# A decoder layer between its first layer norm and its feed-forward: where the sums of the Strassen operands run, how many pairs begin ahead, when the first weights are split, and how many buffers the norm's output has

## The chip, the cores and the metric

The kernel runs on one core of one Trainium2 chip. The metric is device time in microseconds (us) of one execution, the median of three runs. TensorE (PE) does the matrix products, VectorE (DVE) and ScalarE (ACT) the elementwise work, GpSimd (POOL) a little of it, and SyncE (SP) issues nearly all transfers.

## The reference

One layer of a hybrid decoder on 1056 tokens (1024 of a prompt and 32 of samples), 1024 wide, in float32. Attention and an mLSTM head group come first; the change lies behind them:

```python
mixed = jnp.concatenate([h_ml, o_nsa], axis=-1) @ w_out
x = layer_norm(ALPHA * x + g1 * mixed, ln_g[0], ln_b[0])
u2 = x * (1 + sc2) + sh2
ff = jnp.square(jax.nn.relu(u2 @ w_up)) @ w_down
x = layer_norm(ALPHA * x + g2 * ff, ln_g[1], ln_b[1])
```

`w_up` is 1024 x 4096 and `w_down` 4096 x 1024.

## The kernel before, in words

**Precision.** TensorE multiplies in a reduced float32. Each operand is therefore split into a high and a low part (`split`, L50 and L51: ScalarE rounds the high part, VectorE subtracts it from the source), and each product is three products: high by high, high by low, low by high.

**Norm.** Tokens are worked in three chunks `c` of 384, 384 and 288. `wout_steps(c)` multiplies the mixed heads by `w_out`; `ln1(c)` turns the result by TensorE transposes (`pn`), normalises it by rows (`xn`), turns it back (`pb`), scales it on ScalarE into a tile `x1` of two rotating buffers (L1303), stores that (`d_x1`, L1304) for the second residual, and makes `u2` from it in `uraw` (L1307 to L1310). Then it splits the quarters of `uraw` that are operands as they stand.

**Feed-forward up.** `u2 @ w_up` is done by a Strassen-Winograd scheme: two halves of the features by two halves of the tokens give the blocks B11, B21 and B22 and the sums T1 to T4, and seven products make a pair `p` of weight tiles (16 pairs; one weight tile is 512 KB). Two of the seven take B11 and B21 alone, and need no sum:

```python
def first_products(p, ra, v1):
    for x, of in multiply(p, 1, w_of(p, "11", ra[:, 0:4]), "B11"):
        ACT.copy(of(v1), x)
    combine(p, v1, multiply(p, 2, w_of(p, "12", ra[:, 4:8]), "B21"), 0, 0)
```

The other five, in `up_pair`, take T2, T1, T3, B22 and T4 in that order. The sums are T3 = B22 - T3's own quarter, T2 = T3 + its quarter, T4 = its quarter - T2, T1 = B22 - T2, each in place in `uraw`. Before, T3 and T2 are made inside `ln1` for chunks 1 (on GpSimd, 240 columns) and 2 (on VectorE, 288 columns); T4 and T1 later, whole (528 columns, four instructions each), on GpSimd (`TENG`, L1364 records all of them). `t_step` makes and splits one of the four operands.

**Pairs begun ahead.** Of the first `NF` = 4 pairs the two products without a sum are done ahead: those of pairs 0 and 1 inside the norm (`up_early`, with weights split there), those of pairs 2 and 3 after it (`up_start`, tile names `wpre` and `aws`), each followed by a `t_step`. Their result `V1` goes to memory (`d_v1`) and is read again when the pair's other five products run; their weight tile is read again too. `wpre`, the weights of pair 2, is loaded early, but split after the norm into tiles (`a`, four buffers each of high and low) of a pool that opens when the norm's pools close. Other weight tiles share three buffers (`aw`).

**Order.** Instructions are emitted in the order of the program; at build a planner with a simulated time line may start a later one earlier on an engine that would stand idle, and so fixes one order for each engine's queue and for SP's transfers. That is why rows of one line are interleaved with rows of others below.

Of the kernel before, what the change touches and what calls it, by code (L numbers as in the profile page):

```python
# [22 lines left out]
F32 = mybir.dt.float32  # L23
F32R = mybir.dt.float32r
# [12 lines left out]
EPS = 1e-5  # L37
GC = math.sqrt(2.0 / math.pi)
TH, HH = T // 2, T // 4
NF = 4  # L40
KT, B22L = 0, True
NE = 2


# [3 lines left out]
def split(nc, hi, lo, src):  # L48

    nc.scalar.copy(hi, src)  # L50
    nc.vector.tensor_tensor(out=lo, in0=src, in1=hi.bitcast(F32), op=ALU.subtract)  # L51


def body(tc, io, dbg=None):
    with ExitStack() as top:
        _body(tc, tc.nc, top, io, dbg or {})


def _body(tc, nc, top, io, dbg):
    PE, ACT, DVE, POOL, SP = nc.tensor, nc.scalar, nc.vector, nc.gpsimd, nc.sync  # L60

    def pool(name, stack, bufs=1, space=None, side=None):
        kw = {}
        if space is not None:
            kw["space"] = space
        if side is not None:
            kw["side"] = side
        if space is not DRAM:
            kw["reuse_waits"] = "tile"
        return stack.enter_context(tc.tile_pool(name=name, bufs=bufs, **kw))  # L70

    def mk(p, shape, dt, tag, bufs=None, name=None):
        kw = {} if bufs is None else {"bufs": bufs}
        return p.tile(list(shape), dt, tag=tag, name=name or tag, **kw)
# [16 lines left out]
    def v4(x, t=4):  # L91
        return x.rearrange("p (b t) -> p b t", t=t)

    def bc(x, n):

        return x.unsqueeze(2).broadcast_to([x.shape[0], x.shape[1], n])
# [729 lines left out]
    for h in range(2):  # L826
# [23 lines left out]
        for j in range(2):  # L850
            o, p = 512 * j, 288 * j
# [321 lines left out]
    while not (qs.end and qp.end and dn_end):  # L1173
# [4 lines left out]
        if best <= t and (behind or dn_at > t):  # L1178
            if rp <= t:
                qp.need = None  # L1180
                c = qp.pull()
            else:
                qs.need = None
                c = qs.pull()
# [4 lines left out]
        elif dn_at <= t:  # L1189
            x = next(dense, None)  # L1190
# [6 lines left out]
        else:  # L1197
            if fill is None and heads_done[0] and filled < 2 and blocks_done[0] >= 11 + 3 * filled:
                fill = wout_steps(filled)
            if fill is not None:  # L1200
                x = next(fill, None)
# [25 lines left out]
    ops = {}  # L1227

    def operand(pp, name):
        ops[name] = tuple(mk(pp, [128, 4, TH], F32R, name + x) for x in "hl")  # L1230
# [8 lines left out]
    p4 = pool("p4", s4_, side="right")  # L1239
# [20 lines left out]
    def norm_rows(pp, pts, name, cols, rows):  # L1260

        xn, st = norm_tiles(pp, name)
        for hf in range(2):
            norm_half(pts, st, cols, hf, rows)
        _, r, nmr = norm_stats(st, rows)
        for hf in range(2):
            ACT.activation(xn[0:rows, 512 * hf:512 * hf + 512], pts[hf][0:rows], AF.Identity, scale=r, bias=nmr)
        return xn
# [22 lines left out]
    def ln1(c):  # L1291
        t0, n = CH[c]
        tts = [(o, min(128, n - o)) for o in range(0, n, 128)]
        xns = []
        for o, rows in tts:
            pts = [mk(ps4, [128, 512], F32, "t", bufs=4, name=f"pn{c}{o}{hf}") for hf in range(2)]
            xns.append(norm_rows(p4, pts, f"a{c}{o}", [ys[c, m][:, o:o + rows] for m in range(8)], rows))
        for f in range(8):
            pt = mk(ps4, [128, 512], F32, "t2", bufs=2, name=f"pb{c}{f}")
            for (o, rows), xn in zip(tts, xns):  # L1300
                PE.transpose(pt[:, o:o + rows], xn[0:rows, 128 * f:128 * f + 128], ident[0:rows, 0:rows])
            x1 = mk(p4, [128, 384], F32, "x1", bufs=2, name=f"x1{c}{f}")
            ACT.activation(x1[:, 0:n], pt[:, 0:n], AF.Identity, scale=lnT[:, 0, f:f + 1], bias=lnT[:, 1, f:f + 1])  # L1303
            SP.dma_start(d_x1[:, f, t0:t0 + n], x1[:, 0:n])  # L1304
            u = uraw[:, f, t0:t0 + n]
            np_ = min(n, 1024 - t0)
            DVE.tensor_scalar(u[:, 0:np_], x1[:, 0:np_], sc2p[:, f, 0:1], ada[:, 3, f, 0:1], op0=ALU.mult, op1=ALU.add)  # L1307
            if np_ < n:
                DVE.tensor_tensor(out=v4(u[:, np_:n]), in0=v4(x1[:, np_:n]), in1=bc(sc2p[:, f, 1:9], 4), op=ALU.mult)
                DVE.tensor_tensor(out=v4(u[:, np_:n]), in0=v4(u[:, np_:n]), in1=bc(ada[:, 3, f, 1:9], 4), op=ALU.add)  # L1310
            for a, b, name in ((t0, min(t0 + n, TH), "B21" if f >= 4 else "B11"), (max(t0, TH), t0 + n, "B22")):
                if a < b and (a < TH or f >= 4 and c < 2):
                    hi, lo = (x[:, f % 4, a % TH:a % TH + b - a] for x in ops[name])
                    split(nc, hi, lo, uraw[:, f, a:b])
            if f >= 4 and c:
                a, b = ((0, 240), (240, TH))[c - 1]
                t_sum("T3", f - 4, a, b, POOL if c == 1 else DVE)
                t_sum("T2", f - 4, a, b, POOL if c == 1 else DVE)
                if c == 2 and f < 4 + KT:
                    split(nc, ops["T2"][0][:, f - 4], ops["T2"][1][:, f - 4], ublock("T2", f - 4, 0, TH))  # L1320

    d_r = [mk(dr, [128, 2, T], F32, f"d_r{p}") for p in range(16)]
    d_v1 = [mk(dr, [128, TH], F32, f"d_v1{p}") for p in range(NF)]

    def product(ps, w, name, h):

        for i, (a, b) in enumerate(((0, 0), (0, 1), (1, 0))):
            for k in range(4):
                PE.matmul(ps[:, 0:HH], lhsT=w[a][:, k], rhs=ops[name][b][:, k, HH * h:HH * h + HH],  # L1329
                          start=(i == 0 and k == 0), stop=(i == 2 and k == 3))  # L1330
# [19 lines left out]
    def relu2(x):  # L1350
        DVE.scalar_tensor_tensor(out=x, in0=x, scalar=0.0, in1=x, op0=ALU.max, op1=ALU.mult)
# [6 lines left out]
    def ublock(name, k, a, b):  # L1358
        f, t = blk[name]
        return uraw[:, f + k, t + a:t + b]  # L1360

    def t_sum(name, k, a, b, eng):
        x, y, op = sum_of[name]
        eng.tensor_tensor(out=ublock(name, k, a, b), in0=ublock(x, k, a, b), in1=ublock(y, k, a, b), op=op)  # L1364

    TENG = POOL
    ln1(0)
    for _ in fill or wout_steps(1):
        pass
    ln1(1)  # L1370
    for _ in wout_steps(2, pq):
        pass
    operand(pq, "T2")
    ln1(2)
    spre = ExitStack()
    ppre = pool("pre", spre)
    wpre = mk(ppre, [128, 8, 128], F32, "wpre")
    if NF > NE:
        SP.dma_start(wpre, io["w_up"][2 * NE].rearrange("p (k c) -> p k c", k=8))
    for p in range(NE):  # L1380
        up_early(p)
    s4_.close()
# [13 lines left out]
        operand(pT, name)  # L1396

    def t_split(name, a=0):
        for k in range(KT if name == "T2" else 0, 4):
            split(nc, ops[name][0][:, k, a:], ops[name][1][:, k, a:], ublock(name, k, a, TH))  # L1400

    ns = [0]
# [1 line left out]
    def slot(name):  # L1404

        ns[0] += 1
        if ns[0] % 2:
            t = mk(psd, [128, 2, 512], F32, "d", bufs=2, name=name)
            return [t[:, h] for h in range(2)], [(t[:, :, 0:HH], lambda x: x.rearrange("p (h c) -> p h c", h=2))]
        ts = [wtile(f"{name}{h}") if ns[0] % 4 else mk(psd, [128, 512], F32, "t", bufs=2, name=f"{name}{h}") for h in range(2)]  # L1410
        return ts, [(t[:, 0:HH], lambda x, h=h: x[:, HH * h:HH * h + HH]) for h, t in enumerate(ts)]

    def w_of(p, name, src):
        hl = [mk(pU, [128, 4, 128], F32R, "a" + x, bufs=4, name=f"a{x}{p}{name}") for x in "hl"]
        split(nc, *hl, src)
        return hl

    def multiply(p, name, w, op):
        ps, pieces = slot(f"p{name}{p}")
        for h in range(2):  # L1420
            product(ps[h], w, op, h)
        return pieces

    def add(out, v, ps):
        for x, of in ps:
            DVE.tensor_tensor(out=of(out), in0=of(v), in1=x, op=ALU.add)

    def combine(p, v, ps, f, half):

        c = mk(pU, [128, TH], F32, "C", bufs=2, name=f"C{p}{f}{half}")  # L1430
        add(c, v, ps)
        relu2(c)
        SP.dma_start(d_r[p][:, f, TH * half:TH * half + TH], c)

    def first_products(p, ra, v1):
        for x, of in multiply(p, 1, w_of(p, "11", ra[:, 0:4]), "B11"):
            ACT.copy(of(v1), x)
        combine(p, v1, multiply(p, 2, w_of(p, "12", ra[:, 4:8]), "B21"), 0, 0)

    def up_start(p):  # L1440
        ra = wpre
# [7 lines left out]
    def up_pair(p):  # L1449
# [5 lines left out]
        def tile_(tag, bufs=1):  # L1455
            return mk(pU, [128, TH], F32, tag, bufs=bufs, name=f"{tag}{p}")

        v1 = tile_("V1", 2)
        if p < NF:
            SP.dma_start(v1, d_v1[p])  # L1460
# [15 lines left out]
    def t_step(op):  # L1476
        if op == "T1" and B22L:
            t_split("B22", 240)
        if op not in ("T2", "T3"):
            for k in range(4):  # L1480
                t_sum(op, k, 0, TH, TENG)
        t_split(op)

    steps = ["T2", "T3", "T4", "T1"]
    for p in range(NE, NF):
        up_start(p)
        if steps:
# [380 lines left out]
```

## Time and profile before

| | |
|---|---|
| median of three runs | 1561.07 us (1560.75 to 1563.67) |
| profiled execution, its own time | 1566.92 us |
| its span | 1565.1 us |
| mean granted TensorE clock | 0.981 of full speed |
| TensorE busy | 95% of the span |

The profiled execution is 5.85 us longer than the median of the runs, and 1.8 us of its time lie outside the span. A busy TensorE row is modelled time: two rows overlap at their ends, and at a low granted clock the same matmul is longer.

### The profile page before, as it was taken

The page shows a single profiled execution, that of the slowest core. Times are in us where ns is not written, and L with a number is a line of the kernel's source. Part 1 is how long each engine was busy: PE and PEld are TensorE (multiplying, and loading weights), DVE is VectorE, ACT ScalarE, POOL GpSimd, SP SyncE. Part 2 cuts the span into 40 slices and gives each one's busy share as a digit, 9 for nine tenths or more (in the row PEclk, how much of TensorE's full clock was granted, in tenths as well). Part 3 has the DMA queues.
Part 4 walks back from the last instruction along what each step waited for, and adds up shares of the span by engine and source line. Part 5 has one row for each costly group of instructions (what it writes and reads, how often), then busy time and mean ns, then how long its engine had stood idle before and what let it go on. Part 6 is the DMA issues. An engine that isn't in the chain of part 4 may idle for free.

```text
span 1565.1 us, 30108 instructions
## 1 busy us (share of the span) xinstructions
PE 1491.6 (95%) x11647; PEld 1434.5 (92%) x11647; DVE 1029.1 (66%) x2347; ACT 657.3 (42%) x1332; POOL 254.3 (16%) x386
## 2 busy tenths in 40 slices
PE   6899999999999999999998799999999999999985
PEld 5789988899999998798897799999999999999984
DVE  2521131386676777977688887667668687879856
ACT  2422132375565666745366422222225533334443
POOL 0000000143223233443102400000000000002132
PEclk9999999999999999999999799999999999999998
DMA  8766576421020323233464476333324452526473
GB/s 301 272 212 243 134 195 224 146 67 59 26 78 18 82 82 121 80 66 107 155 214 143 164 233 207 125 110 109 105 82 142 141 166 71 150 97 138 111 133 112
DMA packets 115722, 212.04 MB, mean 135 GB/s; under 512 B 18834, under 2 KB 63803, under 8 KB 114651
## 3 DMA queue, kind: packets, MB, share of 16 engines
q1 hardware_dynamic: 109242, 196.67, 39.0%
q0 software_dynamic: 5040, 12.13, 4.7%
q8 instruction: 92, 1.51, 0.4%
q10 hardware_dynamic: 1296, 1.31, 0.2%
q14 instruction: 52, 0.42, 0.1%
HBM read 162.95 MB, written 46.07 MB: 134 GB/s over the span
## 4 chain that ended last, share of the span: by engine, by line
PE 80%; DMA 8%; DVE 6%; issue 2%; ACT 2%; SPq 1%; POOL 0%; ACTq 0%; DVEq 0%; POOLq 0%
PE p L1329 20%; PE pd L1564 18%; PE pj L354 16%; PE po L354 6%; PE o L1060 4%; PE pt L1019 4%; PE S L979 4%; DMA wada<-in_w_ada 3%; DMA xk<-in_xT 1%; PE pA L298 1%; PE ada L149 1%; PE pd L1664 1%; DMA xnf<-ln 1%; PE hidS L277 1%; PE S L983 1%
## 5 line engine op out<-in xcount | busy, mean ns | idle before, releaser
L1564 PE MATMUL pd<-oplT,ophT 128*128 128x264 f32 x2352 | 288.3, 285 | 0.0
L1564 PEld LDWEIGHTS pd<-oplT,ophT 128*128 128x128 f32 x2352 | 288.0, 188 | 0.1
L1002 POOL TENSOR_SCALAR P<-P,l,sg 128x64 f32<-128x64 f32 (+8 forms) x192 | 128.2, 681 | 178.2 <-DVE l L999 159.4
L996 ACT ACTIVATE P<-P,mn 128x640 f32<-128x640 f32 (+7 forms) x128 | 94.3, 737 | 69.8 <-DVE mn L823 66.3
L51 DVE TENSOR_TENSOR PTl<-pt,PTh 128x512 fp32r<-128x512 f32 (+1 forms) x160 | 101.7, 642 | 28.7 <-ACT PTh L50 28.4
L354 PE MATMUL pj<-uh,wt_l 128*128 128x384 f32 (+1 forms) x576 | 120.2, 333 | 0.0
L50 ACT CAST PTh<-pt 128x512 fp32r<-128x512 f32 (+1 forms) x160 | 86.5, 549 | 78.6 <-PE pt L1019 77.9
L354 PE MATMUL pj<-uh,wt_h 128*128 128x384 f32 (+1 forms) x576 | 115.8, 331 | 1.7 <-ACT rw L468 1.7
L354 PE MATMUL pj<-ul,wt_h 128*128 128x384 f32 (+1 forms) x576 | 116.3, 329 | 0.0
L50 ACT CAST ophT<-A 128x1024 fp32r<-128x1024 f32 x49 | 51.2, 1049 | 117.5 <-PE pd L1564 107.4
L354 PEld LDWEIGHTS pj<-uh,wt_l 128*128 128x128 f32 x576 | 95.6, 190 | 2.9 <-issue 2.4
L354 PEld LDWEIGHTS pj<-uh,wt_h 128*128 128x128 f32 x576 | 93.5, 188 | 4.2 <-ACT rw L468 2.0
L1019 PE MATMUL pt<-ident,P 128*128 128x128 f32 x592 | 95.9, 276 | 1.1 <-POOL P L1002 1.0
L354 PEld LDWEIGHTS pj<-ul,wt_h 128*128 128x128 f32 x576 | 94.4, 188 | 1.9 <-issue 1.4
L1615 POOL DMA_DIRECT2D A<-A x7 | 6.3, 895 | 525.4 <-DVE ophT L51 525.4
L1569 DVE TENSOR_TENSOR acc<-acc,pd 128x264 f32<-128x264 f32 (+1 forms) x126 | 62.0, 514 | 28.5 <-PE pd L1564 28.3
L1060 PE MATMUL o<-PTh,V 128*128 128x256 f32 x264 | 79.2, 307 | 0.4 <-DVE ob L1079 0.4
L1060 PE MATMUL o<-PTl,V 128*128 128x256 f32 x264 | 72.7, 296 | 3.1 <-DVE PTl L51 2.7
L1019 PEld LDWEIGHTS pt<-ident,P 128*128 128x128 f32 x592 | 70.4, 141 | 4.3 <-POOL P L1002 1.8
L979 PE MATMUL S<-K,QH 128*128 128x512 f32 (+3 forms) x200 | 71.9, 363 | 0.9 <-DVE mn L823 0.7
L51 DVE TENSOR_TENSOR ophT<-A,ophT 128x1024 fp32r<-128x1024 f32 x49 | 59.6, 1219 | 11.5 <-ACT ophT L50 11.5
L50 ACT CAST ah<-aw 128x512 fp32r<-128x512 f32 x40 | 24.8, 621 | 94.4 <-PE p L1329 94.4
(1104 smaller groups left out, 3473.2 us busy)
## 6 DMA issues: line engine op xcount, KB each, us to landing
wada<-in_w_ada SPq DMA_DIRECT2D x48, 512.0 KB
aw<-in_w_up SPq DMA_DIRECT2D x32, 512.0 KB
d_r<-C SPq DMA_DIRECT2D x62, 264.0 KB
B<-d_r SPq DMA_DIRECT2D x28, 528.0 KB
A<-in_w_down SPq DMA_DIRECT2D x28, 512.0 KB
wst<-in_w_t SPq DMA_DIRECT2D x24, 512.0 KB
wst<-in_w_out SPq DMA_DIRECT2D x24, 512.0 KB
w<-in_cmp_w SPq DMA_DIRECT2D x4, 1024.0 KB
```

The source lines that it names most:

```text
L50: nc.scalar.copy(hi, src)
L51: nc.vector.tensor_tensor(out=lo, in0=src, in1=hi.bitcast(F32), op=ALU.subtract)
L149: PE.matmul(ps[32 * j:32 * j + 32, 0:128], lhsT=sil[:, k, :], rhs=w[:, k % 2, j], start=(k == 0), stop=(k == 7), tile_position=(0, 32 * j))
L354: PE.matmul(ps[:, 0:n], lhsT=a[:, k, :], rhs=b[:, k, t0:t0 + n], start=(i == 0 and k == 0), stop=(i == 2 and k == 7))
L979: PE.matmul(S[:, 0:w], lhsT=Q[:, r], rhs=K[j][:, k0 + c0:k0 + c0 + w], start=(i == 0), stop=(i == 1))
L996: ACT.activation(P[:, o:o + n], P[:, o:o + n], AF.Exp, bias=mn[:, br:br + 1], scale=-1.0, accum_out=l[:, br:br + 1])
L1002: POOL.tensor_scalar(P[:, a:b], P[:, a:b], l[:, x:x + 1], sg[:, qb, y:y + 1], op0=ALU.mult, op1=ALU.mult)
L1019: PE.transpose(pt[:, 256 * x + 128 * e:256 * x + 128 * e + 128], P[:, o:o + 128], ident)
L1060: PE.matmul(op, lhsT=vv, rhs=ps[e][:, 256 * x:256 * x + 256], start=(x0 + x == 0 and e == 0), stop=(x0 + x == len(bl) - 1 and e == 1))
L1329: PE.matmul(ps[:, 0:HH], lhsT=w[a][:, k], rhs=ops[name][b][:, k, HH * h:HH * h + HH], start=(i == 0 and k == 0), stop=(i == 2 and k == 3))
L1564: PE.matmul(ps[h][:, 0:HH], lhsT=x[:, 128 * m:128 * m + 128], rhs=y[:, HH * h:HH * h + HH], start=(i == 0), stop=(i == len(mms) - 1))
L1569: DVE.tensor_tensor(out=out, in0=out, in1=x, op=ALU.add)
```

## The change

Operand sums leave GpSimd: T3 and T2 are no longer made inside `ln1` but after it, in two pieces each on VectorE, and T4 and T1 are made on VectorE. `NF` becomes 6, so that the first two products of pairs 2 to 5 are done ahead of pair 0's other five. `wpre` is emitted before the norm, and its split, as one instruction on ScalarE and one on VectorE into tiles of its own, before the norm's last chunk. `x1` has six buffers in place of two. The order of the operands becomes T2, T1, T3, T4, the order in which the pair uses them. (`KT` was 0, so its lines did nothing.)

```diff
-NF = 4
-KT, B22L = 0, True
+NF = 6
+B22L = True
...
-            x1 = mk(p4, [128, 384], F32, "x1", bufs=2, name=f"x1{c}{f}")
+            x1 = mk(p4, [128, 384], F32, "x1", bufs=6, name=f"x1{c}{f}")
...
-            if f >= 4 and c:
-                a, b = ((0, 240), (240, TH))[c - 1]
-                t_sum("T3", f - 4, a, b, POOL if c == 1 else DVE)
-                t_sum("T2", f - 4, a, b, POOL if c == 1 else DVE)
-                if c == 2 and f < 4 + KT:
-                    split(nc, ops["T2"][0][:, f - 4], ops["T2"][1][:, f - 4], ublock("T2", f - 4, 0, TH))
...
-    TENG = POOL
+    TENG = DVE
+    spre = ExitStack()
+    ppre = pool("pre", spre)
+    wpre = mk(ppre, [128, 8, 128], F32, "wpre")
+    SP.dma_start(wpre, io["w_up"][2 * NE].rearrange("p (k c) -> p k c", k=8))
     ln1(0)
...
     operand(pq, "T2")
+    wpre_hl = [mk(ppre, [128, 8, 128], F32R, "wpre" + x) for x in "hl"]
+    split(nc, *wpre_hl, wpre)
     ln1(2)
-    spre = ExitStack()
-    ppre = pool("pre", spre)
-    wpre = mk(ppre, [128, 8, 128], F32, "wpre")
-    if NF > NE:
-        SP.dma_start(wpre, io["w_up"][2 * NE].rearrange("p (k c) -> p k c", k=8))
+    for k in range(4):
+        for a, b in ((0, 240), (240, TH)):
+            t_sum("T3", k, a, b, DVE)
+            t_sum("T2", k, a, b, DVE)
     for p in range(NE):
         up_early(p)
...
-        for k in range(KT if name == "T2" else 0, 4):
+        for k in range(4):
...
-        for x, of in multiply(p, 1, w_of(p, "11", ra[:, 0:4]), "B11"):
+        wa, wb = ([x[:, 4 * y:4 * y + 4] for x in wpre_hl] if p == NE else w_of(p, "1%d" % (y + 1), ra[:, 4 * y:4 * y + 4])
+                  for y in range(2))
+        for x, of in multiply(p, 1, wa, "B11"):
             ACT.copy(of(v1), x)
-        combine(p, v1, multiply(p, 2, w_of(p, "12", ra[:, 4:8]), "B21"), 0, 0)
+        combine(p, v1, multiply(p, 2, wb, "B21"), 0, 0)
...
-    steps = ["T2", "T3", "T4", "T1"]
+    steps = ["T2", "T1", "T3", "T4"]
```

## Rows read from the trace of the kernel before

**Rows 1.** The page: the span, TensorE's busy time, and its granted clock in 40 slices of the span (tenths of full speed).
```profile
span 1565.1 us, 30108 instructions
PE 1491.6 (95%) x11647; PEld 1434.5 (92%) x11647; DVE 1029.1 (66%) x2347; ACT 657.3 (42%) x1332; POOL 254.3 (16%) x386
...
PEclk9999999999999999999999799999999999999998
```

**Rows 2.** Four long stretches (us from the span's start): length, busy time and count of instructions of each engine, the granted TensorE clock, the transfers' share, and GB/s.
```profile
780.00:835.00 55.00, 55.00 (x406) 54.87 (x405) 45.26 (x98) 33.53 (x50) 3.48 (x6) 1.00 0.62 197
835.00:891.00 56.00, 40.46 (x245) 36.27 (x244) 49.36 (x109) 31.55 (x64) 28.94 (x19) 0.82 0.35 119
891.00:950.00 59.00, 59.00 (x483) 59.00 (x483) 46.01 (x83) 12.23 (x21) 0.00 (x0) 1.00 0.74 243
891.00:1200.00 309.00, 309.00 (x2527) 309.00 (x2527) 226.69 (x394) 77.73 (x129) 1.07 (x1) 1.00 0.41 138
```

**Rows 3.** The same inside the second of these stretches: its three parts, and two pieces of 5 us.
```profile
835.00:858.00 23.00, 19.46 (x127) 16.27 (x125) 18.49 (x58) 15.43 (x34) 7.80 (x11) 0.93 0.39 131
858.00:862.00 4.00, 0.31 (x3) 0.13 (x1) 4.00 (x6) 2.73 (x6) 2.87 (x3) 0.82 0.24 78
862.00:891.00 29.00, 20.68 (x117) 19.86 (x118) 26.87 (x47) 13.39 (x26) 18.27 (x6) 0.74 0.34 114
...
880.00:885.00 5.00, 0.96 (x5) 0.65 (x3) 3.69 (x5) 2.39 (x4) 5.00 (x4) 0.84 0.25 73
885.00:890.00 5.00, 3.57 (x16) 3.57 (x17) 4.87 (x9) 3.21 (x6) 0.19 (x1) 0.50 0.56 188
```

**Rows 4.** Who waited for whom from 830 to 895 us: us in total, times, longest.
```profile
ACT T4h L50 <- POOL uraw L1364: 9.5, 2, 8.9
...
PE p L1329 <- ACT ah0s L50: 5.5, 1, 5.5
...
PE p L1329 <- ACT ah L50: 3.8, 1, 3.8
...
PE p L1329 <- DVE al L51: 2.8, 2, 2.5
...
ACT x L1303 <- DMA d_x<-x: 1.8, 2, 1.2
```

**Rows 5.** GpSimd's groups from 835 to 891 us: shapes and count, then busy us, mean ns of one, and idle time before them.
```profile
L1364 POOL TENSOR_TENSOR uraw<-uraw 128x528 f32<-128x528 f32 x8 | 21.1, 2669 | 16.7 <-DVE uraw L1364 16.7
L1364 POOL TENSOR_TENSOR uraw<-uraw 128x240 f32<-128x240 f32 x8 | 5.7, 727 | 0.4
```

**Rows 6.** VectorE's groups of the same stretch, in the same columns.
```profile
L1364 DVE TENSOR_TENSOR uraw<-uraw 128x288 f32<-128x288 f32 x8 | 4.5, 585 | 0.0
L1307 DVE TENSOR_SCALAR uraw<-x,sc2p,adaT 128x256 f32<-128x256 f32 x8 | 4.3, 534 | 3.5 <-ACT x L1303 3.4
L51 DVE TENSOR_TENSOR T4l<-uraw,T4h 128x528 fp32r<-128x528 f32 x4 | 4.1, 1026 | 2.0 <-ACT T4h L50 1.9
...
L51 DVE TENSOR_TENSOR T3l<-uraw,T3h 128x528 fp32r<-128x528 f32 x4 | 2.8, 691 | 0.0
L51 DVE TENSOR_TENSOR B21l<-uraw,B21h 128x144 fp32r<-128x144 f32 x4 | 2.7, 668 | 0.0
...
L51 DVE TENSOR_TENSOR B22l<-uraw,B22h 128x240 fp32r<-128x240 f32 x4 | 2.6, 642 | 0.0
...
L1351 DVE SCALAR_TENSOR_TENSOR c11e<-c11e 128x264 f32<-128x264 f32 x1 | 1.5, 1524 | 0.0
L1426 DVE TENSOR_TENSOR C<-V1s,p 128x264 f32<-128x264 f32 x4 | 1.5, 418 | 0.0
L1351 DVE SCALAR_TENSOR_TENSOR C<-C 128x528 f32<-128x528 f32 x2 | 1.4, 696 | 0.0
L51 DVE TENSOR_TENSOR al<-wpre,ah 128x512 fp32r<-128x512 f32 x2 | 1.4, 676 | 0.0
```

**Rows 7.** The tile `uraw` over the whole span: shortest, median and longest ns of each group, its first and last start.
```profile
L1307 DVE TENSOR_SCALAR uraw<-x,sc2p,adaT x24: 401/468/1406, 805.2 to 864.8; 128x384 f32<-128x384 f32 x16, 128x256 f32<-128x256 f32 x8
L1364 POOL TENSOR_TENSOR uraw<-uraw x16: 693/1028/10784, 839.4 to 883.4; 128x240 f32<-128x240 f32 x8, 128x528 f32<-128x528 f32 x8
...
L51 DVE TENSOR_TENSOR B21l<-uraw,B21h x8: 242/553/811, 818.8 to 846.7; 128x384 fp32r<-128x384 f32 x4, 128x144 fp32r<-128x144 f32 x4
...
L51 DVE TENSOR_TENSOR B22l<-uraw,B22h x8: 385/446/895, 841.0 to 872.1; 128x240 fp32r<-128x240 f32 x4, 128x288 fp32r<-128x288 f32 x4
...
L1309 DVE TENSOR_TENSOR uraw<-x,sc2p x8: 176/183/1304, 848.1 to 865.1; 128x32 f32<-128x32 f32 x8
...
L1364 DVE TENSOR_TENSOR uraw<-uraw x8: 443/448/1552, 857.1 to 869.6; 128x288 f32<-128x288 f32 x8
```

**Rows 8.** TensorE's time line: start, length, name, count, and in brackets the idle time before it and what ended it. The first row is a run of eight transposes and the second what starts behind it; the last is pair 0's first product with a sum.
```profile
831.53 1.04 PE L1245 MATMUL pn<-ident,y 128*128 128x128 f32 x8
832.33 0.74 PE L1329 MATMUL pu0e<-B11h,wu0h 128*128 128x264 f32 x4
...
886.43 1.25 PE L1329 MATMUL p<-T2h,ah0s 128*128 128x264 f32 x4 [5.47 <-ACT ah0s L50]
```

**Rows 9.** SP's transfers: start, length of the issue, and the tile, for the weights of pair 3 and of pair 0.
```profile
862.72 0.38 SPq L1444 DMA_DIRECT2D aws<-in_w_up  x1
863.15 0.92 SPq L1452 DMA_DIRECT2D aw<-in_w_up  x2
```

## The prediction

> **What bounds the kernel now.** I read the page first: TensorE is busy for 95% of the span, and its granted clock dips in one slice alone, just past the middle [rows 1]. The long stretches show what lies there. From 891 us on TensorE never idles: 2527 instructions in 309.0 us, 122.3 ns each, at the full clock [rows 2]; time is saved there only by taking matmuls away, and the change takes none. The 56.0 us from 835 to 891 are another thing: 40.46 us busy, with a granted clock of 0.82 [rows 2]. Of the 245 instructions there 197 are matmuls of 264 columns (counted by groups) and 48 are transposes, which take 0.10 us each (eight in 0.80 us, [rows 8]). At the full rate that is 197 x 0.1223 + 48 x 0.10 = 28.9 us of work, so 27.1 us are lost: 8.5 until 858 (23 us for 80 matmuls and 47 transposes), 3.9 from 858 to 862, and 14.7 in the last 29 us (117 matmuls, 14.3 us of work) [rows 3]. This is the most that the change can win here. Part of it is clock: TensorE ran 0.96 us of the 5 from 880, and the next 5 us were granted 0.50, the 1.2 GHz level [rows 3].
>
> The waits say who was late. TensorE waited 5.5 us for ScalarE's split of pair 0's weights, 3.8 us for that of `wpre`, 2.8 us for VectorE's low parts; behind the first stands ScalarE, which waited 9.5 us for GpSimd's sums of T4 [rows 4]. GpSimd took 21.1 us for eight sums of 528 columns, one of them 10.784 us long [rows 5, 7]. The reader is to see that the sums, not the products, set pair 0's start at 886.43 us [rows 8].
>
> **The sums on VectorE.** They have two prices. VectorE pays for the work: eight sums of 528 columns at 0.69 us (its splits of that size, T3l, [rows 6]) are 5.5 us, and eight of 240 columns at 0.385 us (the shortest B22l, [rows 7]) are 3.1 us. And it gets time back, because its own instructions were stretched while GpSimd's sums ran. Against the undisturbed row of the same size: T4l 4 x (1.026 - 0.691) = 1.3; B21l 4 x (0.668 - 0.242) = 1.7; B22l 4 x (0.642 - 0.385) = 1.0; the 288-column sums 8 x (0.585 - 0.448) = 1.1; L1307 8 x (0.534 - 0.401) = 1.1; one L1309 1.304 - 0.183 = 1.1; c11e at least 1.524 - 0.696 = 0.8 (the 696 ns are for twice the columns) [rows 6, 7]. Together 8.1 us. So the sums cost VectorE 0.5 us net, and the 9.5 us wait behind GpSimd goes. VectorE's own idle 1.9 us before T4l [rows 6] goes with it.
>
> Here a rule speaks against the change. The Trainium skill, page Perfetto Trace Analysis, section Optimizing Scalar/DVE Operations, says that where VectorE is saturated it may pay to move work off it, even to GpSimd, and warns that the two share a port, so that it may not help. By the first half the move would cost 8.6 us and the gain below would fall to about 5; the rows bear out the warning, and the sum goes by them.
>
> **Four pairs in place of two.** Two more pairs do 96 matmuls ahead, 11.7 us of TensorE work at 0.1223 us. They are moved, not added: pairs 4 and 5 are shorter by as much later on. What they bring is cover while the sums are made. VectorE does with them 2 x (2 x 0.676 + 2 x 0.418 + 0.696) = 5.8 us more in the stage (low parts of two weight tiles, sums with V1, the squared relu, [rows 6]). Added outright are transfers: per pair one weight tile read twice (0.52 MB) and V1 stored and read (0.27 MB each), 2.1 MB for both. In the stage the transfers' share is 0.35, and 0.74 in the 59 us behind it with TensorE never idle [rows 2], so I cost them at nothing; if that cover were gone, 2.1 MB at the 243 GB/s of that row would be 8.7 us.
>
> **The early split and the six buffers.** The split of `wpre` leaves the stage: 2 x 0.676 = 1.4 us of VectorE [rows 6] fall before 835, where VectorE has 9.7 us idle of 55 and ScalarE 21.5 [rows 2]. TensorE's 3.8 us wait for it [rows 4] gets pair 2's products as filler. The six `x1` buffers take away ScalarE's 1.8 us of waits for stores of `x1` [rows 4], and VectorE idles 3.4 us for these same ScalarE outputs [rows 6]; I take the 1.8 off VectorE's idle time (bounds 0 and 3.4). The order T2, T1, T3, T4 is the order of use, costs nothing, and lets T4 be late.
>
> **The sum.** The work up to the same point (pair 0's first two sum-products done) took before 56.0 us, and with the two more pairs it would be 56.0 + 11.7 = 67.7. After, TensorE needs at least 28.9 + 11.7 = 40.6 us of this, and VectorE is the longer: 49.4 - 8.1 + 5.5 + 3.1 + 5.8 - 1.4 = 54.3 us busy. Its idle time was 6.6 us [rows 2]; less 1.9 and 1.8 it is 2.9, so 57.2. But T4 is used last by pair 0, so that its four sums and four splits (5.5 us) may lie behind this point; between all and none I take half, 2.8, since the other splits also wait their turn: 54.4 us. The gain is 67.7 - 54.4 = 13.3 us. The profiled execution of 1566.9 would become 1553.6; taken off the median, 1561.1 becomes 1547.8 us. With no deferral and nothing from `x1` VectorE takes 59.0 and the gain is 8.7 (1552.4); with all deferred and 1.0 us of idle it takes 49.8 and the gain is 17.9 (1543.2). That is this case's own range.
>
> **Rivals.**
> *VectorE's queue is in the wrong order.* T1's sums and splits (8 x 0.69 = 5.5 us) stand ahead of pair 4's low parts in the program, T3's splits (2.8 us) ahead of pair 5's. If TensorE has run out of products then, it loses 8.3 us and the gain is 5.0: 1556.1 us. For it: the 2.8 us wait for low parts now, and VectorE at 88% of the stage [rows 2, 4]. Against: pairs 2 and 3 give 11.7 us of cover, and a planner that fills gaps need not keep the order. The skill's rule above ends near this time.
>
> *TensorE becomes the bound.* If VectorE's lateness is all hidden, the loss up to 858 alone stays: 28.9 + 11.7 + 8.5 = 49.1, a gain of 18.6: 1542.5. For it: VectorE idles 4.5 us of 23 before 858 [rows 3], room for sums. Against: it was full from 858 to 862 and worked 26.87 of the last 29 us.
>
> *The weights come too late, so nothing is won.* Pairs 3 to 5 and pair 0 need five tiles through three `aw` buffers; before, three were asked for from 862.72 on [rows 9]. If each must be waited for in turn, 0.52 MB at 243 GB/s is 2.2 us; three of them and pair 0's two make 10.9 us, and the gain is 2.4: 1558.7. Against: that stage's transfers stand at 0.34 [rows 3].
>
> *Slower: the short pairs starve.* Pairs with five products take 120 x 0.1223 = 14.7 us of TensorE and, by the stretch from 891 to 950 (four such pairs), 46.0 / 4 = 11.5 us of VectorE. There are six of them now, VectorE enters them with T3 and T4 still to do, and the first operands of the down product are loaded at the same time. This decides from a pair of 17.4 us on: 2.7 us lost in each of six eats the 13.3 and 3.1 more. With 17.5 the time is 1564.6. Against: in the four before, TensorE was busy for 59.00 of 59.00 us.
>
> **How the numbers follow.** The likeliest case has 0.59, the queue's order 0.18, TensorE as the bound 0.10, late weights 0.08, starving pairs 0.05. 0.2% is 3.1 us, about what a measurement of this kernel can tell from no change. Faster by more than that: the first three, less 0.03 for the low end of the second, 0.84; within it 0.10; slower 0.06. The range from 1542.0 to 1557.5 leaves out half of the TensorE case and the last two.
>
> **What would show it.** GpSimd has only the norm's small powers left; no VectorE row of the stage is stretched over 0.75 us for up to 528 columns; no 9.5 us wait of ScalarE. The `wpre` split lies before 835, pair 2's matmuls fill the gap at 858. TensorE's instructions behind the norm are 192 of `p` before the first T2, with waits of a few us for low parts and a first T2 product at about 884. The granted clock of the stage is above 0.9. Wrong would be: a new wait over 5 us for `aw`, gaps behind 891, or VectorE idle while TensorE waits.

## The result, and the profile after

The change made the kernel faster by less than forecast: 1551.73 us median (1550.44 to 1555.08, 5 runs) against 1562.41 us (1560.75 to 1563.67, 5 runs) for the kernel before on the same chip. The ratio is 0.994, with a 95% interval from 0.9919 to 0.9962, so the gain is between 5.9 and 12.7 us. The profiled execution took 1554.74 us, with a span of 1553.0 us. Forecast were 1547.8 us, in a range from 1542.0 to 1557.5. In the table of the experiments, one execution of the kernel with the early split alone (1618.09 us at a granted clock of 0.88) was a slow one and is left out of its median.

The page of the kernel after; the rows answer to [rows 1], and the dip of the granted clock in the middle is gone:

```profile
span 1553.0 us, 30101 instructions
PE 1488.8 (96%) x11647; PEld 1431.3 (92%) x11647; DVE 1027.6 (66%) x2363; ACT 656.9 (42%) x1330; POOL 230.1 (15%) x370
...
PEclk9989999999999999999999999999999999999998
```

The long stretches of the kernel after, in the columns of [rows 2]:

```profile
780.00:835.00 55.00, 52.87 (x389) 52.59 (x387) 44.38 (x100) 32.22 (x47) 5.35 (x7) 1.00 0.61 193
835.00:891.00 56.00, 48.02 (x334) 44.19 (x335) 49.08 (x126) 36.38 (x72) 2.40 (x2) 0.93 0.49 161
891.00:950.00 59.00, 59.00 (x478) 59.00 (x477) 50.35 (x90) 12.23 (x20) 0.00 (x0) 0.98 0.76 267
891.00:1200.00 309.00, 309.00 (x2524) 309.00 (x2523) 233.02 (x398) 82.67 (x138) 1.07 (x1) 1.00 0.43 147
```

In the 56 us from 835 TensorE does 334 instructions where it did 245, at a clock of 0.93 where it had 0.82. One thing is worse: before 835 it was never idle, now it loses 2.1 us there. The waits from 830 to 895 us, against [rows 4]:

```profile
ACT ah0s L50 <- DVE s L1465: 3.6, 1, 3.6
PE p L1323 <- ACT ah L50: 3.4, 1, 3.4
PE pb L1301 <- ACT xna L1267: 3.1, 2, 2.2
...
ACT x L1303 <- PE pb L1301: 2.8, 1, 2.8
...
PE p L1323 <- ACT ah0s L50: 2.0, 1, 2.0
```

ScalarE waits for GpSimd no more, nor for stores of `x1`. The first row is the wait that stands now where GpSimd stood: ScalarE can split pair 0's first weights (`ah0s`) only when VectorE has made their sum `s`. GpSimd has two powers of the norm left in these 56 us, and the tile `uraw`, in the columns of [rows 7], shows no stretched row:

```profile
L1307 DVE TENSOR_SCALAR uraw<-x,sc2p,adaT x24: 408/470/480, 811.2 to 864.4; 128x384 f32<-128x384 f32 x16, 128x256 f32<-128x256 f32 x8
L1358 DVE TENSOR_TENSOR uraw<-uraw x24: 378/458/720, 841.1 to 880.8; 128x240 f32<-128x240 f32 x8, 128x288 f32<-128x288 f32 x8, 128x528 f32<-128x528 f32 x8
```

**The measure for the parts.** The profiled executions differ by some us in places that the change does not touch: the last product of attention (`o`) starts between 775.6 and 783.8 us in them, and the part from the first down product (`pd`) to the end takes from 368.28 to 371.11. What lies between, from the start of that last `o` (taken to a tenth of a us) to the first start of `pd`, holds the whole change. I call it the stage. In two executions of one kernel it came within 0.44 us (402.72 and 402.28); its parts repeat less well, for pair 0 starts 93.2 and 94.1 us behind `o` in them, and the rest takes 309.50 and 308.21. Inside the stage a difference of a us therefore tells nothing. It took 412.69 us before (781.30 to 1193.99) and takes 404.36 after (779.60 to 1183.96): 8.3 us gained. The prediction's 13.3 us were counted on this stage, so it was 5.0 too high there. The two profiled spans differ by 12.1 us; the other 3.8 arose outside the stage. Every gain is counted from the one profiled execution of the kernel before; differences among the other kernels do not depend on it.

### The profile page after: what moved, and what is told of

It reads as the page before. It is cut to its first block, busy times and chain, and to the rows that moved or that the text cites. A ratio compares the mean times of both kernels' runs of the same rounds, so it can differ in the third digit from the quotient of the medians.

```text
span 1553.0 us, 30101 instructions
## 1 busy us (share of the span) xinstructions
PE 1488.8 (96%) x11647; PEld 1431.3 (92%) x11647; DVE 1027.6 (66%) x2363; ACT 656.9 (42%) x1330; POOL 230.1 (15%) x370
## 4 chain that ended last, share of the span: by engine, by line
PE 74%; DMA 9%; DVE 7%; issue 5%; ACT 2%; POOL 2%; SPq 1%; DVEq 0%; POOLq 0%; ACTq 0%
PE p L1323 19%; PE pj L354 16%; PE pd L1565 13%; PE po L354 6%; PE o L1060 4%; PE pt L1019 4%; PE S L979 4%; DMA wada<-in_w_ada 3%; PE pA L298 1%; PE ada L149 1%; DMA wa<-in_w_a 1%; DMA wst<-in_w_t 1%; POOL acc L1592 1%; DMA kvr<-in_cache_c 1%; DMA xnf<-ln 1%
## 5 line engine op out<-in xcount | busy, mean ns | idle before, releaser
L1425 DVE TENSOR_TENSOR V<-V,p 128x264 f32<-128x264 f32 (+1 forms) x72 | 37.3, 520 | 41.6 <-PE p L1323 41.4
```

## The experiments

Stage lengths are from the one profiled execution of each run. Times are medians, and ratios are to the kernel before, run beside it. The intervals of the ratios overlap for most pairs of kernels, so the stage carries the argument and the times only have to agree with it. They do, with two small exceptions: for "before + six" the stage gains 6.4 us and the ratio says 7.3 to 14.2, and for "after, four" 5.7 against 6.1 to 12.3.

| kernel | time, us | ratio, 95% | stage, us |
|---|---|---|---|
| after | 1551.73 | 0.9919 to 0.9962 | 404.36 |
| before + sums | 1553.79 | 0.9907 to 0.9956 | 402.72, 402.28 |
| before + six | 1552.62 | 0.9909 to 0.9953 | 406.32 |
| before + sums and six | 1548.32 | 0.9880 to 0.9941 | 398.16 |
| before + early split | 1564.81 | 1.0010 to 1.0046 | 419.40 |
| after, T1 and T4 sums on GpSimd | 1555.33 | 0.9931 to 0.9971 | 407.25 |
| after, four | 1554.71 | 0.9921 to 0.9961 | 407.04 |
| after, two `x1` buffers | 1551.15 | 0.9897 to 0.9952 | 404.54 |
| after, split behind the norm | 1546.52 | 0.9862 to 0.9921 | 398.34 |
| after, split held | 1551.29 | 0.9915 to 0.9961 | 404.25 |
| after, products held | 1552.47 | 0.9909 to 0.9957 | 403.80 |
| after, both held | 1548.52 | 0.9855 to 0.9942 | 398.02 |

"Four" and "six" are the values of `NF`: two of these pairs are computed outright inside the norm, so they are two and four pairs begun ahead.

**The sums alone, in the kernel before.**

```diff
-    TENG = POOL
+    TENG = DVE
-                t_sum("T3", f - 4, a, b, POOL if c == 1 else DVE)
-                t_sum("T2", f - 4, a, b, POOL if c == 1 else DVE)
+                t_sum("T3", f - 4, a, b, DVE)
+                t_sum("T2", f - 4, a, b, DVE)
```

> The kernel before with all its operand sums on VectorE and nothing else changed. Theory A: the 9.5 us wait behind GpSimd goes, VectorE's stretched 8.1 us come back against 8.6 us of sums: 5 to 8 us won, 1554 to 1557 us. Theory B: without more cover TensorE waits for VectorE in place of GpSimd, at most 2 us won, 1559 to 1562 us.

Measured: 402.72 us, 10.0 less than before: more than the 5 to 8 expected, and more than the whole change wins. The stretches of the kernel before, from 53.7 us behind `o` to pair 0's first product, and from there to `pd`:

```profile
835.00:886.43 51.43, 35.89 (x224) 31.70 (x223) 44.79 (x100) 29.55 (x61) 28.94 (x19) 0.85 0.33 114
...
886.43:1193.99 307.56, 307.56 (x2496) 307.56 (x2497) 225.25 (x396) 76.20 (x128) 0.82 (x1) 0.99 0.41 138
```

The same two with the sums on VectorE:

```profile
830.20:869.72 39.52, 31.60 (x224) 28.00 (x222) 36.89 (x107) 27.85 (x58) 2.31 (x3) 0.96 0.46 156
...
869.72:1179.22 309.50, 307.39 (x2496) 306.97 (x2497) 230.73 (x405) 78.04 (x131) 1.07 (x1) 0.99 0.40 136
```

VectorE does 16 instructions more (107 + 405 against 100 + 396, all the sums), and yet it is busy 267.62 us in place of 270.04. The sums were priced at 8.6 us (and took 8.7), so about 11.0 us of stretched time came back. In the first stretch it is busy 7.9 us less and idle 4.0 less (6.64 to 2.63), and that is the 11.9 us by which pair 0 starts sooner. Behind it, 5.5 us of VectorE work are made up, TensorE stands 2.1 us (it is busy 307.39 of 309.50), and that stretch is 1.9 us longer.

> A second run of the kernel before with its sums on VectorE and nothing else changed, to see how far one profiled execution repeats: the stage from o to the first down product again within 0.7 us of 402.7 if the stage is set by the fixed order of the queues; otherwise the differences of 2 us between variants mean nothing.

This label names six pairs, but the kernel run under it is the one above, unchanged. It serves as its repeat: 402.28 us. VectorE is busy 267.42 us in it, idle 3.60 in the first stretch, and the second stretch is 0.6 us longer than before, so the 4.0 and the 1.9 above are rough.

**Four pairs ahead alone, in the kernel before.**

```diff
-NF = 4
+NF = 6
```

> The kernel before with six pairs begun ahead in place of four and nothing else changed; sums stay on GpSimd. Theory A: ScalarE still stands behind GpSimd's sums, and with it the splits of the further pairs' weights: 0 to 3 us won, 1558 to 1562 us. Theory B: the cover hides GpSimd's sums, 7 to 10 us won, 1551 to 1555 us.

Measured: 406.32 us, 6.4 less, which lies between the two theories. GpSimd's sums are still there, up to 8966 ns for one, and ScalarE still waits 7.7 us for them; more of it is covered.

**The sums and four pairs, without the rest.** The two diffs above together.

> The kernel before with its sums on VectorE, inside the norm as they stood, and six pairs begun ahead; old order, old split, two x1 buffers. If cover and sums add up, the two gaps of 2.4 and 1.8 us of the sums-only kernel at pair 0 close: stage 398 to 401, time 1549 to 1552 us. If VectorE is the bound there, the stage stays at 402 to 404, as with the sums alone.

Measured: 398.16 us, 14.5 less than before: 10.2 by the sums (mean of two runs) and 4.3 by the pairs on top. These two parts of the change, without the others, would have gained 6.2 us more than the change does.

**T1 and T4's sums back on GpSimd, in the kernel after.**

```diff
-    TENG = DVE
+    TENG = POOL
```

> The changed kernel with T4's and T1's eight sums of 528 columns back on GpSimd; the rest as changed. Theory A (the sums' place carries the gain: VectorE stretched by GpSimd, ScalarE held behind GpSimd): VectorE's rows are stretched again, ScalarE waits over 4 us for GpSimd, and 5 to 9 us of the gain of about 10 are lost: 1557 to 1561 us. Theory B (the cover of the two more pairs carries it): the sums on GpSimd lie under the 23 us of first products, VectorE is spared 5.5 us, and the time stays within 2 us of the changed kernel, 1550 to 1553 us.

Measured: 407.25 us, 2.9 more, which lies between the two theories. The tile `uraw` (shortest, median and longest ns) shows both engines' rows stretched:

```profile
L1358 DVE TENSOR_TENSOR uraw<-uraw x16: 378/422/1583, 838.1 to 873.8; 128x240 f32<-128x240 f32 x8, 128x288 f32<-128x288 f32 x8
...
L1358 POOL TENSOR_TENSOR uraw<-uraw x8: 1317/1598/1857, 858.7 to 876.0; 128x528 f32<-128x528 f32 x8
...
L51 DVE TENSOR_TENSOR T4l<-uraw,T4h x4: 691/695/1827, 868.6 to 883.8; 128x528 fp32r<-128x528 f32 x4
```

VectorE has eight instructions fewer than in the kernel after and is busy 1.5 us longer (269.92 us from 53.7 us behind `o` to `pd`, against 268.39). The Trainium skill, page SBUF — State Buffer, section Who interferes with whom, says that a VectorE instruction with two inputs in SBUF contends with a GpSimd instruction that reads SBUF, and calls the ports that the two share an exclusive lock. The rows agree: a split of 691 ns becomes one of 1827 ns, longer by 1.1 us, somewhat less than one GpSimd sum (1.3 to 1.9 us).

**Two pairs ahead, in the kernel after.**

```diff
-NF = 6
+NF = 4
```

> The changed kernel with only two pairs begun ahead after the norm (4 in all), the rest as changed. Theory A: VectorE has 5.8 us less to do in the stage, so pair 0 starts some 6 us earlier in work of VectorE, and TensorE waits for the remainder of 11.7: 3 to 6 us lost, 1554 to 1558 us. Theory B (cover carries it): 8 to 10 us lost, 1560 to 1562 us.

Measured: 407.04 us. Here the two more pairs are worth 2.7 us, a little under the 3 to 6 expected by theory A.

**Two buffers for `x1`, in the kernel after.**

```diff
-            x1 = mk(p4, [128, 384], F32, "x1", bufs=6, name=f"x1{c}{f}")
+            x1 = mk(p4, [128, 384], F32, "x1", bufs=2, name=f"x1{c}{f}")
```

> The changed kernel with two x1 buffers in place of six. Theory C: the late norm comes from the split, so its last x1 stays at about 82 us after o or goes to 84, ScalarE waits again 2 us for stores of x1, stage 404 to 406. Theory E (the six buffers themselves, by the order that the planner makes with them, delay the norm: its first x1 starts 29.6 us after o, 22.8 before): first x1 at 22 to 24, last at 75 to 78, stage 401 to 403.

Measured: 404.54 us against 404.36, which is inside the repeat. The buffers are worth nothing that shows. As theory C had it, the first row stays at 29.6 us and the norm ends later, at 84.8.

**The first weights split behind the norm, in the kernel after.** The early load stays, and the split is made by `w_of` again, as for the other pairs.

```diff
-    wpre_hl = [mk(ppre, [128, 8, 128], F32R, "wpre" + x) for x in "hl"]
-    split(nc, *wpre_hl, wpre)
...
-        wa, wb = ([x[:, 4 * y:4 * y + 4] for x in wpre_hl] if p == NE else w_of(p, "1%d" % (y + 1), ra[:, 4 * y:4 * y + 4])
+        wa, wb = (w_of(p, "1%d" % (y + 1), ra[:, 4 * y:4 * y + 4])
```

> The changed kernel with the split of wpre back behind the norm, in the tiles of the pool that opens there; the load of wpre stays ahead of the norm. Measured as the time from the last attention product (o) to the first product of the down stage: 412.7 us before, 404.4 changed, 402.7 with the sums on VectorE alone. Theory C (the early split lets pair 2's products go ahead of the norm's last transposes, and so the norm's last x1 comes 82 us after o in place of 77): x1 ends at 75 to 78, stage 401 to 403. Theory D (the split fills the gap and its loss shows): a gap of 3 to 4 us before pair 2's first product, stage 406 to 408.

Measured: 398.34 us, under what either theory expected. The early split costs 6.0 us. What is left of the change then equals the sums and pairs alone (398.16), so the order of T1 to T4, the place of the sums behind the norm and the six buffers come to nothing together. On the stage this kernel beats both of the case's. Its time of 1546.52 us agrees, though the interval of its ratio just touches that of the kernel after.

**The early split alone, in the kernel before.** Load and split as in the change, and nothing else of it.

> The kernel before with the early load and the early split of wpre alone; sums, pairs and buffers as before. Theory F: the first x1 comes 28 to 30 us after o in place of 22.8, the norm's end is 4 to 6 us late, the 3.75 us gap before pair 2 is filled but the stage grows from 412.7 to 415 to 419 us, time 1564 to 1569 us. Rival: by itself it wins the gap, stage 409 to 411, time 1558 to 1561 us.

Measured: 419.40 us, 6.7 more than before. It costs about as much without the other parts as with them. The norm ends 88.8 us behind `o` in place of 77.9, which is 11 us late where 4 to 6 were expected, and TensorE stands 5.50 us before pair 0.

**Why it costs: two traces.** The early split stands in ScalarE's queue where the weights have not yet landed. ScalarE's time line in the kernel after:

```profile
788.54 1.05 ACT L50 CAST wpreh<-wpre 128x1024 fp32r<-128x1024 f32 x1 [4.83 <-DMA wpre<-in_w_up]
```

The first normalised rows come 29.6 us behind `o`, against 22.8 with the split behind the norm. Later, pair 2's products, which are ready early, stand between the norm's last transposes (`pb`) in TensorE's order. The kernel after:

```profile
855.98 0.65 PE L1323 MATMUL p<-B21h,wpreh 128*128 128x264 f32 x4
...
857.31 0.55 PE L1301 MATMUL pb<-ident,xna 128*128 128x128 f32 x3
...
858.02 0.56 PE L1301 MATMUL pb<-ident,xna 128*128 128x128 f32 x3
858.51 0.75 PE L1323 MATMUL p<-B21h,wpreh 128*128 128x264 f32 x4
...
860.07 1.09 PE L1301 MATMUL pb<-ident,xna 128*128 128x128 f32 x6
...
867.71 0.75 PE L1323 MATMUL p<-B11h,ah 128*128 128x264 f32 x4 [3.40 <-ACT ah L50]
...
889.11 0.79 PE L1323 MATMUL p<-T2h,ah0s 128*128 128x264 f32 x4 [2.01 <-ACT ah0s L50]
```

And with the split behind the norm, where 18 of them run in one piece and the gap of about 3 us is that for `wpre` itself:

```profile
850.67 3.69 PE L1301 MATMUL pb<-ident,xna 128*128 128x128 f32 x18
857.53 1.25 PE L1323 MATMUL p<-B11h,ah 128*128 128x264 f32 x4 [3.17 <-ACT ah L50]
...
884.39 0.75 PE L1323 MATMUL p<-T2h,ah0s 128*128 128x264 f32 x4 [0.46 <-ACT ah0s L50]
```

So there are two suspects, the late start of the norm and the products ahead of its end. Three kernels hold the one, the other, or both.

**The split held in ScalarE's order behind the last cast of the output weights.**

```diff
+    held = [i for i in nc.cur_bb.bb.instructions if i.engine == mybir.EngineType.Activation][-1]
+    with tc.issue_after(held):
-    split(nc, *wpre_hl, wpre)
+        split(nc, *wpre_hl, wpre)
```

> The changed kernel with its early split kept, but held in ScalarE's order behind the last weight split of the norm's stage (wo27), so that it can't stand ahead of the norm's first rows. Stage from o to the first down product: 404.4 us changed, 398.3 without the early split. Theory F (the place in the queues is the fault: ScalarE waits 4.8 us there for the weights and VectorE's subtraction stands ahead of the row statistics): first x1 again 22 to 23 us after o, the 3.2 us gap before pair 2's first product closes, stage 394 to 397, time 1543 to 1547 us. Theory C (pair 2's products ahead of the norm's last transposes are the fault, wherever the split stands): last x1 at 79 to 82 us after o, stage 402 to 405.

Measured: 404.25 us. The first rows are back at 22.8 us, and nothing is won, where theory F expected 394 to 397. To take away the late start alone wins nothing: the products ahead of the norm's last transposes are enough to cost 5.9 us (404.25 against 398.34).

**The same, and pair 2's products held behind the norm's last transpose.**

```diff
     ln1(2)
+    last_pb = [i for i in nc.cur_bb.bb.instructions if i.engine == mybir.EngineType.PE][-1]
...
-        first_products(p, ra, v1)
+        with tc.issue_after(last_pb) if p == NE else ExitStack():
+            first_products(p, ra, v1)
```

> The changed kernel with the early split held behind the last cast of the output weights in ScalarE's order (as in the run that held the split alone), and with pair 2's products held in TensorE's order behind the third norm's last transpose. Stage from the last attention product to the first down product: 404.36 us in the changed kernel, 404.25 with the split held alone, 398.34 with the split behind the norm. Theory 'products ahead of the norm's end': the 6.0 us are lost because pair 2's products, ready early, stand between the norm's last transposes, so that its last normalised rows come 82 (changed) and 78.5 us (split held) after the last attention product instead of 74, and pair 3's weights, whose load is queued behind the stores of these rows, 9 us late. Then with both held the last rows come at 74 to 77 us, TensorE's gap of 3.1 us in front of pair 3's products is gone, and the stage is 394 to 399 us, time 1542 to 1548 us. Rival 'the split itself': the 1.2 us on VectorE and the cast on ScalarE, standing in the norm's second half, move everything behind them, wherever the products stand; then the rows' end is again near 78 us and the stage 402 to 405 us, time 1549 to 1553 us.

Measured: 398.02 us, all of the 6.0 back. The split itself is as long in this kernel and stands inside the norm, so its own work is not what costs.

**The products held alone.** The second diff without the first.

> The changed kernel with pair 2's products held in TensorE's order behind the third norm's last transpose, and the early split left where the change puts it (the first normalised rows then come 29.6 us after the last attention product instead of 22.8). Theory 'products ahead of the norm's end', if it is the whole of it: the last rows come at 75 to 79 us, stage 394 to 399 us, time 1542 to 1548 us, the same as with both held. Rival 'late start of the norm': the 6.8 us by which the split delays the first rows are not made good by the end of the norm; the last rows stay at 79 to 82 us, the stage comes out 2 to 6 us above the run with both held (399 to 405 us), time 1547 to 1553 us.

Measured: 403.80 us; the first rows come at 29.6 us again. So the products are not the whole of it either: the late start by itself is enough too, and either suspect alone costs about what both cost together. What happens at pair 0's start shows where the time goes. The last 30 us before pair 0's first product and the 5 us behind it, first in the kernel with both held:

```profile
857.86:887.86 30.00, 26.59 (x195) 25.51 (x195) 29.97 (x66) 17.61 (x34) 0.00 (x0) 0.94 0.55 185
887.86:892.86 5.00, 5.00 (x41) 5.00 (x42) 3.53 (x6) 2.24 (x4) 0.00 (x0) 1.00 1.02 344
```

With the products held alone:

```profile
859.68:889.68 30.00, 25.08 (x197) 24.06 (x196) 29.94 (x64) 17.90 (x34) 0.00 (x0) 0.98 0.58 194
889.68:894.68 5.00, 5.00 (x22) 5.00 (x23) 4.82 (x9) 1.60 (x3) 0.00 (x0) 0.50 0.96 317
```

With the split held alone:

```profile
862.16:892.16 30.00, 22.15 (x172) 21.13 (x171) 29.94 (x64) 17.77 (x34) 0.00 (x0) 0.98 0.58 190
892.16:897.16 5.00, 5.00 (x22) 5.00 (x23) 4.82 (x9) 1.61 (x3) 0.00 (x0) 0.50 0.88 292
```

The kernel after:

```profile
859.11:889.11 30.00, 24.59 (x184) 23.74 (x182) 29.87 (x64) 18.15 (x35) 0.00 (x0) 0.94 0.55 183
889.11:894.11 5.00, 5.00 (x28) 5.00 (x29) 3.53 (x6) 1.86 (x4) 0.00 (x0) 0.66 0.94 329
```

The kernel after with two `x1` buffers:

```profile
858.08:888.08 30.00, 26.80 (x203) 26.18 (x202) 30.00 (x66) 18.33 (x35) 0.00 (x0) 0.94 0.54 177
888.08:893.08 5.00, 5.00 (x44) 5.00 (x42) 3.68 (x7) 1.44 (x3) 0.00 (x0) 1.00 0.94 315
```

VectorE is full in all five (29.87 to 30.00 of 30 us): what the norm's last rows release, it works off until pair 0 can start, and the products of the pairs are the cover. Its last rows before that, in the kernel after:

```profile
885.85 0.72 DVE L51 TENSOR_TENSOR T1l<-uraw,T1h 128x528 fp32r<-128x528 f32 x1
886.47 0.72 DVE L51 TENSOR_TENSOR T4l<-uraw,T4h 128x528 fp32r<-128x528 f32 x1
887.08 0.72 DVE L1345 SCALAR_TENSOR_TENSOR C<-C 128x528 f32<-128x528 f32 x1
887.70 0.70 DVE L1465 TENSOR_TENSOR s<-s,aw 128x512 f32<-128x512 f32 x1
```

The last row is the `s` for which ScalarE waits 3.6 us. The table gives us behind `o`, from the time lines; the norm's end is that of ScalarE's last normalised row.

| kernel | norm's end | pair 0 starts | TensorE idle before it | granted clock in the next 5 us | from there to `pd` |
|---|---|---|---|---|---|
| split behind the norm | 75.4 | 104.7 | 0.46 | 1.00 | 293.65 |
| both held | 76.5 | 105.4 | 0.22 | 1.00 | 292.66 |
| products held | 79.3 | 108.0 | 3.60 | 0.50 | 295.82 |
| split held | 79.7 | 108.4 | 3.62 | 0.50 | 295.89 |
| after | 82.7 | 109.5 | 2.01 | 0.66 | 294.85 |
| after, two `x1` buffers | 84.8 | 111.1 | 0.00 | 1.00 | 293.46 |

Each late end of the norm is passed on to pair 0, which starts 26 to 29 us behind it in all six, with VectorE idle for 0.1 us of that at the most. On the norm's end the two suspects add up: against both held, the late start alone (products held) costs 2.8 us, the products alone (split held) 3.2, and both (after) 6.2. On the stage they cost 5.8, 6.2 and 6.3. In these three the cover runs out, TensorE stands 2.0 to 3.6 us, and it then goes on at about half its clock, the 1.2 GHz level where 0.50 is shown. In the ten us behind pair 0's start 61 matmuls (products held) or 60 (split held) are done in place of 82 (both held), which at 0.1223 us is 2.6 to 2.7 us. So the 6 us are 2.6 to 4.1 of late start and 2.2 to 3.2 behind it, most of that clock.

The clock behind pair 0 is not a part of the price everywhere: with two `x1` buffers nothing stands there and the clock is 1.00, but pair 0 starts 5.7 us late, and the stage is 6.5 longer than with both held. Common to all is the late end of the norm. Why the four sums come out within 0.7 us of one another these rows do not show.

## Why the prediction was right, and where its sum was not

The time fell into the range and the likeliest case held its sign, but its sum was wrong in both directions, above all by the sums on VectorE and the early split: the first brought 6.0 us more than forecast, all other terms together 11.0 less. That the total missed by no more than 5.0 is luck, since the two offset one another. On the stage the 8.3 us lie just under the low end of 8.7 that the prediction gave. By its own steps, in us gained on the stage:

| term | forecast | measured |
|---|---|---|
| sums on VectorE (8.1 + 1.9 + 2.8 - 8.6) | 4.2 | 10.2 |
| two more pairs (11.7 - 5.8) | 5.9 | 4.3 |
| early split | 1.4 | -6.0 |
| `x1` buffers, order of T1 to T4, place of the sums | 1.8 | -0.2 |
| sum | 13.3 | 8.3 |

- **The sums.** The mechanism was right: the 9.5 us wait and the stretched rows go. The size was off. Stretched time given back was 11.0 in place of 8.1, since I added up only the rows that stood out. VectorE's idle time fell by 4.0 in place of 1.9. Behind pair 0's start came 5.5 us more of VectorE's work, where I took 2.8. The stretch behind it grows by 1.9, which I had not counted: 2.9 + 2.1 + 2.7 - 1.9 is the 5.8 that the single run shows above the forecast.
- **The deferral.** The 2.8 us were the half of T4's sums and splits, since T4 is used last. That is not what happened. With the sums alone, what lies behind pair 0's start is two low parts each of T1, T2 and T4 (T4's at 876.92 and 878.15 us, behind 869.72) and three sums. In the kernel after it is none of them: T4's last low part is made at 886.47, ahead of pair 0. So the order T2, T1, T3, T4 let nothing be late, and this term is 0 there.
- **The rule on saturated engines.** By the first half of what the Trainium skill says (Perfetto Trace Analysis, Optimizing Scalar/DVE Operations) the gain would have been about 5. Its warning on the shared port holds, and more than that: when VectorE took over GpSimd's sums it was busy for 2.4 us less, and when eight of them were given back 1.5 us more.
- **The pairs.** 4.3 on top of the sums, 6.4 while GpSimd still made the sums late, 2.7 beside the early split. Their transfers are hidden as costed: behind 891 us TensorE is busy 309.00 of 309.00 us.
- **The early split** is the step that failed. I moved 1.4 us off VectorE and named the idle time that would hide it (9.7 us of VectorE before 835, 21.5 of ScalarE [rows 2]), but not its place in an in-order queue: ScalarE stands 4.83 us there for weights that are still on their way, ahead of the norm's own work. And I counted the filled 3.8 us gap [rows 4] as good, where it is worth nothing, and the products that were to fill it ran ahead of the norm's last transposes: TensorE's gap was slack, since VectorE set pair 0's start. In the kernel with both held that gap is gone (0.31 us), and its stage of 398.02 us is the same, within the repeat, as the 398.34 of the kernel that has it.
- **The `x1` buffers.** ScalarE's wait for stores went, and it waits 2.8 us for the transposes in its place. What I took off VectorE's idle time was not set by the stores.
- **What was to show it.** Right: GpSimd has only powers left, no row of `uraw` on VectorE is over 0.72 us, the clock from 835 to 891 is 0.93, and nothing starves behind 891. Wrong: pair 0 was to start at about 884 us, and it starts at 889.11, although `o` comes 1.7 us sooner.
- **The rivals.** Late weights show as one gap of 3.40 us in front of pair 3's products. It is 3.10 us with the split held and 0.29 us with the products held, and the stages of these two differ by 0.45 us, so it is slack. TensorE did not become the bound: VectorE is full and TensorE idles 5.4 of the last 30 us before pair 0. The queue's order, at 0.18, stays open. Four low parts of T1 and T4 (0.72 us each, from 883.93 on) stand close ahead of the `s` that pair 0's first product needs, while pair 0 uses T1 second and T4 last. But the same low parts stand ahead of `s` with the split behind the norm too, where TensorE's wait is 0.46 us. So the order does not explain the 6.0 us; what a better one would bring no run shows.

What the runs do not settle: the 3.8 us of the two profiled executions that lie outside the stage lie in parts that the diff does not touch. I take them for the spread between executions, since two executions of one kernel (the sums alone) start their last `o` 5.6 us apart; it was not tested further.

## What to carry to other kernels

Moving work early to fill a gap pays only if that gap's engine is late for the next thing that matters; here the gap was slack, and what was moved stood in front of the chain (norm, then VectorE) that set the next start. A moved instruction costs also what it makes its queue wait for, so look up where its input lands, and hold it back by its engine's order where that is later. When several parts are changed at once, measure the best one alone: here two of them were worth 14.5 us and the whole 8.3.

## What was unexpected of the hardware

Sixteen more instructions on VectorE made it busy for 2.4 us less, because GpSimd's instructions had stretched its own. And in three kernels a stand of 2.0 to 3.6 us of TensorE was followed by 5 us at a granted clock of 0.66 or 0.50, with 0.91 to 1.00 in the 5 us behind these; after 0.22 or 0.46 us of idle time the clock stayed at 1.00. So a start that is 3 us late can cost 6. It does not always come so: in the two executions of the sums alone, 5 us behind stands of 2.38 and 2.51 us were granted 1.00 and 0.71, and the 5 us after those 0.66 and 1.00.
